# A decoder layer on one core: the norm of the retention outputs and the softmax each issued in two steps, and the key transposes in a step of their own

## The chip, the cores and the metric

The kernel runs on one core of one Trainium2 chip. A core has a matrix engine (TensorE, here PE, with its weight loads shown as PEld), a vector engine (DVE), an activation engine (ACT), a general engine (POOL), and SyncE (SP), which only issues transfers; they run side by side and meet through semaphores. The metric is the device time of one execution, in microseconds (us).

## The reference, cut to what matters

One decoder layer is computed for a prompt of 512 tokens and 8 samples of 8 tokens: 576 columns in all, D_MODEL 1024, fp32 throughout. After an RMS norm one combined projection gives the inputs of three branches, each with a norm, a scan or a softmax of its own; their projections are gated and merged, and an MLP and a small gated term follow. The two parts that the change touches are these:

```python
def step(s, inp):                      # retention, one chunk of 128 tokens
    qi, ki, vi = inp
    inner = einsum('bhid,bhjd->bhij', qi, ki) * dmask
    o = einsum('bhij,bhje->bhie', inner, vi) + einsum('bhid,bhde->bhie', qi * q_dec, s)
    s = s * c_dec + einsum('bhjd,bhje->bhde', ki * k_dec, vi)
    return s, o
...
o = o * lax.rsqrt(mean(o * o, axis=-1) + EPS)      # per head
return silu(rg) * o, s
...
m = maximum(max(s, axis=-1), sink)                 # window attention
pr = exp(s - m)
pr = pr / (sum(pr, axis=-1) + exp(sink - m))
```

## The kernel before, in words

Every large product is done in fp32 by splitting both operands into a high and a low part and adding three matmuls. Most of them go through `pair` or `pairs`: a recursive scheme with fewer multiplications whose `product` (L329) is 12 matmuls of 128x128 by 288 columns, accumulated in PSUM banks that the trace names pa, pbb and pe; the rest go through `unit` (`mm`, L501, bank pm). PE is fed with weights that SP loads (`wst`), ACT rounds (`whi`, L256 or L163), and DVE completes (`wlo`, L257 or L164; L227 first forms sums of weight blocks). Results leave PSUM through DVE (L424, L426) and ACT.

The branches' own small work runs in between. It is written as generators in a list `bg`; each `pump()` in `pair` and `unit` advances the first of them by one `yield`, so that a step's instructions are written between two big products. A framework then settles the order on each engine and the semaphores; within an engine that order is fixed. The banks for small work (tile pb) come from the same pool of six as pa and pe, so asking for a bank can wait for whoever reads the one that comes round next.

Retention (`ret_gen`) takes four prompt chunks of 128 tokens. For a chunk: scores (L713) with their decay mask (L717, DVE), transposed keys (L721, PE) with their decay (L723, DVE), decayed queries (L730, DVE, behind a POOL memset L728), outputs po (L737 from the scores and L739 from decayed queries and the state), state update pu (L744, L751). `ret_out` then normalises: squares on ACT, a mean over rows by a matmul (pn, L685), the inverse root (`rsqrt`: transpose L548, add L554, the power on POOL L555, refinement L556, L557, L560, transpose back L562), the gate t1 = po * rg (L690), and the product with the inverse root (L691). Convolution work (L838 to L845) and weight preparation share DVE with it. `stats` uses the same `rsqrt` at the start of the layer, once for each half of the columns; x is then normalised (L587, L653, L642) and made into operands for the pairs (L366, L583).

```python
yield
pk = bank("pb")                  # transposed keys: the bank that it gets is the last chunk's po
...
yield
yield
po = bank("pb")
...
yield
yield
pu = bank("pb")
```

Attention (`att_gen`) computes scores (L947, L952), `softmax` (maximum L892, exponentials L896 on ACT, denominator L899, L900, and eight scalings L902 on DVE), and the values (L972, L974, L964), block by block.

Of the kernel before, what the change touches and what calls it, by code (L numbers as in the profile page):

```python
# [10 lines left out]
ALU = mybir.AluOpType  # L11
AX = mybir.AxisListType

P = 128
# [70 lines left out]
def decoder_step(ctx: ExitStack, tc: tile.TileContext, xT, pT, W, consts, smalls, s0q, s0t, ckT, cv,  # L85
# [38 lines left out]
    def bank(s="ps"):  # L124
        return psum.tile([P, 512], F32, tag="ps", name=nm(s))
# [415 lines left out]
    def gain(i, k):  # L541
        return sm[:, S_G + 8 * i + k:S_G + 8 * i + k + 1]

    def rsqrt(v, w, out, c=1.0):

        nb = w // 32
        t1 = tmpt()
        V.transpose(t1[:, :w], v)  # L548
        tv = t1[:, :w].rearrange("p (b q) -> p b q", q=32)
        a = sml.tile([P, 18], F32, tag="rs_a", name=nm("rs_a"))  # L550
        b = sml.tile([P, 18], F32, tag="rs_b", name=nm("rs_b"))
        d = sml.tile([P, 18], F32, tag="rs_d", name=nm("rs_d"))
        a, b, d = a[:, :nb], b[:, :nb], d[:, :nb]
        V.tensor_scalar(a, tv[:, :, 0], EPS, None, op0=ALU.add)  # L554
        G.tensor_tensor(out=b, in0=a, in1=mhalf[:, :nb], op=ALU.pow)  # L555
        V.scalar_tensor_tensor(d, b, -0.5 * c, b, op0=ALU.mult, op1=ALU.mult)  # L556
        V.tensor_tensor(out=d, in0=d, in1=a, op=ALU.mult)  # L557
        t2 = t1
        t2v = t2[:, :w].rearrange("p (b q) -> p b q", q=32)
        V.scalar_tensor_tensor(t2v, d.unsqueeze(2).to_broadcast([P, nb, 32]), 1.5 * c,  # L560
                               b.unsqueeze(2).to_broadcast([P, nb, 32]), op0=ALU.add, op1=ALU.mult)
        V.transpose(out, t2[:, :w])  # L562

    def stats(sq_sum, rb, i):
        p = bank("pb")
# [111 lines left out]
    def ret_out(po, w, c0):  # L677

        ov = po[:, :4 * w]
        sq = bgtile()  # L680
        A.activation(sq[:, :4 * w], ov, AF.Square)
        yield
        yield
        pn = bank("pb")
        PE.matmul(pn[:, :4 * w], lhsT=ones_h, rhs=sq[:, :4 * w], start=True, stop=True)  # L685
        rs = bgtile()
        rsqrt(pn[:, :4 * w], 4 * w, rs[:, :4 * w], 0.5)
        t1 = bgtile()
        t1v = t1[:, :4 * w].rearrange("p (h i) -> p h i", h=4)
        V.tensor_tensor(out=t1v, in0=ov.rearrange("p (h i) -> p h i", h=4), in1=rg[:, :, c0:c0 + w], op=ALU.mult)  # L690
        V.tensor_tensor(out=ro[:, :, c0:c0 + w], in0=t1v,  # L691
                        in1=rs[:, :4 * w].rearrange("p (h i) -> p h i", h=4), op=ALU.mult)

# [3 lines left out]
    def odd(a, q):  # L697

        return a.rearrange("p (t q i) -> p t q i", t=2, q=2)[:, :, q, :]

    def ret_gen():
        vt = big.tile([P, 4, T], F32, tag="big", name="vt")
        state = None
        for c in range(4):
# [11 lines left out]
            for q in range(2):  # L716
                V.tensor_tensor(out=odd(st, q), in0=pst[q][:, :256].rearrange("p (t i) -> p t i", t=2),  # L717
                                in1=odd(cst[:, C_DMASK:C_DMASK + 512], q), op=ALU.mult)
            pk = bank("pb")
            for hp in range(2):  # L720
                PE.transpose(pk[:, 128 * hp:128 * hp + 128], rk[:, hp, cs], ident)  # L721
# [8 lines left out]
                    V.tensor_tensor(out=odd(qd, h)[hrow(h)], in0=rq[hrow(h), :, cs],  # L730
                                    in1=cst[hrow(h), C_QDEC:C_QDEC + 256].rearrange("p (t i) -> p t i", t=2), op=ALU.mult)
            yield
            yield
            po = bank("pb")
            for h in range(4):
                o = po[:, 128 * h:128 * h + 128]
                PE.matmul(o, lhsT=vc[:, 128 * h:128 * h + 128], rhs=st[:, 128 * h:128 * h + 128], start=True, stop=c == 0)  # L737
                if c:
                    PE.matmul(o, lhsT=state[:, h // 2, :], rhs=qd[:, 128 * h:128 * h + 128], start=False, stop=True)  # L739
            yield  # L740
            yield
            pu = bank("pb")
            for h in range(4):
# [142 lines left out]
    def softmax(sv, nh, sink):  # L886

        mx = mpool.tile([P, 8], F32, tag="mx", name=nm("mx"), bufs=2)[:, :nh]
        nmx = mpool.tile([P, 8], F32, tag="nmx", name=nm("nmx"), bufs=3)[:, :nh]
        den = mpool.tile([P, 8], F32, tag="den", name=nm("den"), bufs=3)[:, :nh]  # L890
        es = mpool.tile([P, 8], F32, tag="es", name=nm("es"), bufs=2)[:, :nh]
        V.tensor_reduce(out=mx, in_=sv, axis=AX.X, op=ALU.max)  # L892
        V.tensor_tensor(out=mx, in0=mx, in1=sink, op=ALU.max)
        V.tensor_scalar(nmx, mx, -1.0, None, op0=ALU.mult)
        for h in range(nh):
            A.activation(sv[:, h, :], sv[:, h, :], AF.Exp, bias=nmx[:, h:h + 1], accum_out=den[:, h:h + 1])  # L896
        V.tensor_tensor(out=es, in0=sink, in1=nmx, op=ALU.add)
        A.activation(es, es, AF.Exp)
        V.tensor_tensor(out=den, in0=den, in1=es, op=ALU.add)  # L899
        V.reciprocal(den, den)  # L900
        for h in range(nh):
            V.tensor_scalar(sv[:, h, :], sv[:, h, :], den[:, h:h + 1], None, op0=ALU.mult)  # L902

    def att_inputs():
        akv = bigt(F32, "akv")
# [18 lines left out]
    def att_gen(ak, av, avt, aq):  # L924
# [13 lines left out]
        def scores(n):  # L938
# [4 lines left out]
            for t in range(0, 4, 2):  # L943
# [8 lines left out]
                        V.scalar_tensor_tensor(s[:, h, :], dist, -SLOPES[h], p[g][:, i * w:i * w + w],  # L952
                                               op0=ALU.mult, op1=ALU.add)
                yield
            softmax(s, 8, sink)
            return s

        def values(n, s):
            nk = 1 if n == 0 else 2
# [29 lines left out]
                      in_=aq[:, :, NP:].rearrange("p t (b i) -> p t b i", b=8))  # L989
        yield  # L990
        sq = [bgtile()[:, :384].rearrange("p (n k) -> p n k", n=2) for _ in range(2)]
        for q in range(2):
            p = bank("pb")
            for n in (2 * q, 2 * q + 1):
# [6 lines left out]
                for j in range(4):  # L1001
# [7 lines left out]
            V.tensor_tensor(out=sq[q][:, :, 128:], in0=pq[:, :, 128:],  # L1009
                            in1=cst[:, C_ATTS + 128 + 128 * q:C_ATTS + 256 + 128 * q].rearrange("p (n k) -> p n k", n=2),  # L1010
                            op=ALU.add)
            softmax(sq[q], 2, sm[:, S_SINKS:S_SINKS + 1].to_broadcast([P, 2]))
            yield
        yield
        pt = bank("pb")
        for n in range(4):
# [24 lines left out]

        prev = None
        for n in range(4):
            s = yield from scores(n)
            if prev is not None:
                yield from values(n - 1, prev)
            prev = s
        yield from values(3, prev)

# [440 lines left out]
```

## Time and profile before

| what | value |
|---|---|
| time, median of 3 runs | 986.15 us (986.05 to 987.69) |
| the profiled execution: its time, its span | 987.22 us, 985.4 us |
| mean granted TensorE clock | 0.994 of full |
| busy in the span: PE, DVE, ACT, POOL | 957.6, 712.6, 531.5, 187.1 us |
| busy share: PE, DVE, ACT, POOL | 97%, 72%, 54%, 19% |
| chain of work that ended last, by engine | PE 77%, DVE 13%, DMA 4%, ACT 2% |

Busy is the time in which an engine had an instruction in work. The chain is followed back from the last instruction, at each step to what released it, so its shares say what set the end. A granted clock of 1 is 2.4 GHz and 0.5 is 1.2 GHz.

### The profile page before, as it was taken

The page shows a single profiled execution, that of the slowest core. Times are in us where ns is not written, and L with a number is a line of the kernel's source. Part 1 is how long each engine was busy: PE and PEld are TensorE (multiplying, and loading weights), DVE is VectorE, ACT ScalarE, POOL GpSimd, SP SyncE. Part 2 cuts the span into 40 slices and gives each one's busy share as a digit, 9 for nine tenths or more (in the row PEclk, how much of TensorE's full clock was granted, in tenths as well). Part 3 has the DMA queues.
Part 4 walks back from the last instruction along what each step waited for, and adds up shares of the span by engine and source line. Part 5 has one row for each costly group of instructions (what it writes and reads, how often), then busy time and mean ns, then how long its engine had stood idle before and what let it go on. Part 6 is the DMA issues. An engine that isn't in the chain of part 4 may idle for free.

```text
span 985.4 us, 18290 instructions
## 1 busy us (share of the span) xinstructions
PE 957.6 (97%) x7081; PEld 925.0 (94%) x7081; DVE 712.6 (72%) x1308; ACT 531.5 (54%) x1051; POOL 187.1 (19%) x257
## 2 busy tenths in 40 slices
PE   9999999989989999999999999999999999999998
PEld 9999898989979888799999999999999999999897
DVE  7898789765576776577427878558847965785986
ACT  7345444433345564545436455468558845885642
POOL 0414443433324222332001100000010011000010
PEclk9999999999999999999999999999999999999999
DMA  8637565658779665688522532444486368593112
GB/s 301 168 86 199 165 138 146 163 164 220 194 218 248 143 153 153 143 226 252 187 66 71 223 108 100 155 148 145 120 199 192 110 153 222 164 356 109 65 62 79
DMA packets 65576, 160.45 MB, mean 163 GB/s; under 512 B 8089, under 2 KB 11193, under 8 KB 64241
## 3 DMA queue, kind: packets, MB, share of 16 engines
q1 hardware_dynamic: 48672, 114.75, 34.9%
q0 software_dynamic: 16672, 44.48, 21.8%
q8 instruction: 55, 0.90, 0.4%
q14 instruction: 33, 0.26, 0.1%
q10 hardware_dynamic: 144, 0.06, 0.0%
HBM read 139.17 MB, written 51.55 MB: 194 GB/s over the span
## 4 chain that ended last, share of the span: by engine, by line
PE 77%; DVE 13%; DMA 4%; ACT 2%; issue 2%; POOL 1%; SPq 0%; ACTq 0%; DVEq 0%; POOLq 0%
PE pm L501 31%; PE pbb L329 18%; PE pa L329 12%; PE pe L329 12%; DMA wst<-in_W 3%; DVE wlo L257 3%; POOL rs_b L555 1%; DVE hlf L1149 1%; DVE xl L579 1%; DVE x L1150 1%; DVE wst L227 1%; DVE s L952 1%; PE pb L964 1%; ACT whi L256 1%; DVE wlo L164 1%
## 5 line engine op out<-in xcount | busy, mean ns | idle before, releaser
L257 DVE TENSOR_TENSOR wlo<-wst,whi 128x1024 fp32r<-128x1024 f32 (+1 forms) x180 | 195.4, 1087 | 95.9 <-ACT whi L256 95.1
L256 ACT CAST whi<-wst 128x1024 fp32r<-128x1024 f32 (+1 forms) x180 | 168.3, 940 | 129.9 <-PE pe L329 29.9
L329 PE MATMUL pbb<-xs,whi 128*128 128x288 f32 x1080 | 227.1, 302 | 10.0 <-DVE akv L426 4.1
L329 PEld LDWEIGHTS pbb<-xs,whi 128*128 128x128 f32 x1080 | 174.9, 190 | 19.0 <-DVE akv L426 4.9
L329 PE MATMUL pbb<-xs,wlo 128*128 128x288 f32 x540 | 160.6, 297 | 0.0
L329 PE MATMUL pa<-fq,whi 128*128 128x288 f32 x720 | 147.7, 297 | 0.6 <-DVE fq L583 0.5
L329 PEld LDWEIGHTS pa<-fq,whi 128*128 128x128 f32 x720 | 116.0, 189 | 2.3 <-DVE fq L583 0.7
L329 PE MATMUL pa<-fq,wlo 128*128 128x288 f32 x360 | 106.8, 297 | 0.4 <-DVE wlo L257 0.4
L329 PEld LDWEIGHTS pbb<-xs,wlo 128*128 128x128 f32 x540 | 102.7, 190 | 0.0
L163 ACT CAST whi<-wst 128x1024 fp32r<-128x1024 f32 (+1 forms) x64 | 61.5, 965 | 70.9 <-PE pm L501 48.8
L501 PE MATMUL pm<-xl,whi 128*128 128x288 f32 x384 | 95.0, 299 | 1.5 <-DVE xl L579 1.4
L501 PE MATMUL pm<-xh,whi 128*128 128x288 f32 x384 | 94.9, 300 | 1.5 <-ACT xh L578 1.4
L501 PE MATMUL pm<-xh,wlo 128*128 128x288 f32 x384 | 93.5, 296 | 0.3 <-DVE wlo L164 0.3
L164 DVE TENSOR_TENSOR wlo<-wst,whi 128x1024 fp32r<-128x1024 f32 (+1 forms) x64 | 71.2, 1118 | 23.7 <-ACT whi L163 21.3
L268 POOL COPY pace<-whi 128x1 f32<-128x1 f32 x61 | 36.6, 600 | 240.8 <-ACT whi L256 190.3
L227 DVE TENSOR_TENSOR wst<-wst 128x512 f32<-128x512 f32 x90 | 61.1, 686 | 28.7 <-DMA wst<-in_W 28.0
L555 POOL TENSOR_TENSOR rs_b<-rs_a,mhalf 128x9 f32<-128x9 f32 (+2 forms) x15 | 34.8, 2322 | 222.7 <-DVE rs_a L554 222.7
L329 PE MATMUL pe<-xs,whi 128*128 128x288 f32 x360 | 73.5, 294 | 0.1
L329 PE MATMUL pe<-fq,whi 128*128 128x288 f32 x360 | 73.3, 296 | 0.0
L501 PE MATMUL pm<-fq,whi 128*128 128x288 f32 x384 | 70.4, 296 | 0.0
L329 PEld LDWEIGHTS pa<-fq,wlo 128*128 128x128 f32 x360 | 67.9, 189 | 1.9 <-DVE wlo L257 1.1
L501 PEld LDWEIGHTS pm<-xh,whi 128*128 128x128 f32 x384 | 65.7, 188 | 3.9 <-ACT xh L578 2.4
(280 smaller groups left out, 2025.6 us busy)
## 6 DMA issues: line engine op xcount, KB each, us to landing
wst<-in_W SPq DMA_DIRECT2D x86, 512.0 KB, 4.5
wst<-in_W SPq DMA_DIRECT2D x105, 256.0 KB, 3.3
ts<-in_W POOLq DMA_DIRECT2D x90, 256.0 KB, 5.7
wst<-ts SPq DMA_DIRECT2D x60, 256.0 KB, 3.3
ts<-ts POOLq DMA_DIRECT2D x30, 256.0 KB, 3.5
df<-tmp POOLq DMA_DIRECT2D x16, 288.0 KB, 5.1
x<-in_xT SPq DMA_DIRECT2D x10, 288.0 KB, 4.2
dacc<-tmp SPq DMA_DIRECT2D x8, 288.0 KB, 4.3
```

What stands on the lines that cost most here:

```text
L163: A.copy(out=hi[:, c, :], in_=st[:, c, :])
L164: V.tensor_tensor(out=lo[:, c, :], in0=st[:, c, :], in1=hi[:, c, :].bitcast(F32), op=ALU.subtract)
L227: V.tensor_tensor(out=out, in0=a, in1=b, op=ALU.add)
L256: A.copy(out=hi, in_=r[:, :n, :])
L257: V.tensor_tensor(out=lo, in0=r[:, :n, :], in1=hi.bitcast(F32), op=ALU.subtract)
L268: t = G.tensor_copy(out=pace, in_=hi[:, 0, :1].bitcast(F32))
L329: PE.matmul(bank[:, :H], lhsT=lhs[:, s + j, :], rhs=rhs, start=start and j == 0 and i == 0, stop=j == 3 and i == 2, skip_group_check=True)
L501: PE.matmul(p[:, :H], lhsT=lhs[:, kw, :], rhs=r, start=s, stop=e)
L555: G.tensor_tensor(out=b, in0=a, in1=mhalf[:, :nb], op=ALU.pow)
L579: V.scalar_tensor_tensor(lo, src, gain(gi, k), hi.bitcast(F32), op0=ALU.mult, op1=ALU.subtract)
L952: V.scalar_tensor_tensor(s[:, h, :], dist, -SLOPES[h], p[g][:, i * w:i * w + w], op0=ALU.mult, op1=ALU.add)
L964: PE.matmul(po[grow(g), :], lhsT=avt[:, 128 * chunk + 64 * g:128 * chunk + 64 * g + 64], rhs=sb[g], start=kh == 0, stop=kh == nk - 1)
```

## The change: what it does

`rsqrt` becomes a generator, `rsqrt_steps`, that stops after the power on POOL; a wrapper `rsqrt` runs it through for `stats`. Its second half writes a tile of its own where it reused the first. `ret_out` runs the first half, then the gate t1, then yields, and does the second half in the next step. In `ret_gen` a `yield` stands ahead of the key transposes, and one is taken away ahead of po and one ahead of pu. `softmax` returns the denominator, the reciprocal and the scalings as a function, `probs()`, that the caller runs later.

```diff
-    def rsqrt(v, w, out, c=1.0):
+    def rsqrt_steps(v, w, out, c=1.0):
...
         G.tensor_tensor(out=b, in0=a, in1=mhalf[:, :nb], op=ALU.pow)
+        yield
         V.scalar_tensor_tensor(d, b, -0.5 * c, b, op0=ALU.mult, op1=ALU.mult)
         V.tensor_tensor(out=d, in0=d, in1=a, op=ALU.mult)
-        t2 = t1
+        t2 = tmpt()
...
+    def rsqrt(v, w, out, c=1.0):
+        for _ in rsqrt_steps(v, w, out, c):
+            pass
...
         rs = bgtile()
-        rsqrt(pn[:, :4 * w], 4 * w, rs[:, :4 * w], 0.5)
+        steps = rsqrt_steps(pn[:, :4 * w], 4 * w, rs[:, :4 * w], 0.5)
+        next(steps)
         t1 = bgtile()
         t1v = t1[:, :4 * w].rearrange("p (h i) -> p h i", h=4)
         V.tensor_tensor(out=t1v, in0=ov.rearrange("p (h i) -> p h i", h=4), in1=rg[:, :, c0:c0 + w], op=ALU.mult)
+        yield
+        for _ in steps:
+            pass
...
+            yield
             pk = bank("pb")
...
             yield
-            yield
             po = bank("pb")
...
-            yield
             yield
             pu = bank("pb")
...
-        V.tensor_tensor(out=den, in0=den, in1=es, op=ALU.add)
-        V.reciprocal(den, den)
-        for h in range(nh):
-            V.tensor_scalar(sv[:, h, :], sv[:, h, :], den[:, h:h + 1], None, op0=ALU.mult)
+
+        def probs():
+            V.tensor_tensor(out=den, in0=den, in1=es, op=ALU.add)
+            V.reciprocal(den, den)
+            for h in range(nh):
+                V.tensor_scalar(sv[:, h, :], sv[:, h, :], den[:, h:h + 1], None, op0=ALU.mult)
+        return probs
...
-            softmax(s, 8, sink)
-            return s
+            return s, softmax(s, 8, sink)
...
-            s = yield from scores(n)
+            s, probs = yield from scores(n)
             if prev is not None:
+                if n == 1:
+                    first_probs()
                 yield from values(n - 1, prev)
+                probs()
+            else:
+                first_probs = probs
```

The sample's softmax is split likewise: the scalings of its first half come after the scores of its second.

The new lines move the numbers: the power stays L555, L556 to L562 become L557 to L563, L587 L592, L690 (the gate) L696, L691 L700, L717 L726, L721 L731, L723 L733, L730 L740, L737 L746, L739 L748, L744 L752, L838 L846, L844 L852.

Order on DVE where the first chunk's norm stands (rs_a, rs_b, rs_d are the small tiles of the inverse root, L690 or L696 the gate). Before:

```order
L548 STREAM_TRANSPOSE tmp_1420<-pb_1417 128x512
L838 TENSOR_TENSOR ubuf_1455<-tmp_1146,tmp_1144 128x512
L554 TENSOR_SCALAR rs_a_1422<-tmp_1420 128x16
L839 TENSOR_TENSOR ubuf_1455<-tmp_1146,tmp_1144 128x8x8
L556 SCALAR_TENSOR_TENSOR rs_d_1424<-rs_b_1423 128x16
L557 TENSOR_TENSOR rs_d_1424<-rs_d_1424,rs_a_1422 128x16
L560 SCALAR_TENSOR_TENSOR tmp_1420<-rs_d_1424,rs_b_1423 128x512
L257 TENSOR_TENSOR wlo_1617<-wst_1611,whi_1616 128x1024
L562 STREAM_TRANSPOSE bgt_1419<-tmp_1420 128x512
L690 TENSOR_TENSOR bgt_1431<-pb_1276,rg_865 128x512
```

After, where the gate has already been done 8 rows above:

```order
L548 STREAM_TRANSPOSE tmp_1384<-pb_1381 128x512
L257 TENSOR_TENSOR wlo_1517<-wst_1420,whi_1516 128x1024
L554 TENSOR_SCALAR rs_a_1386<-tmp_1384 128x16
L426 TENSOR_TENSOR tmp_1149<-hlf_1340,pbb_1313 128x288
L557 SCALAR_TENSOR_TENSOR rs_d_1388<-rs_b_1387 128x16
L227 TENSOR_TENSOR wst_1650<-wst_1614 128x512
L558 TENSOR_TENSOR rs_d_1388<-rs_d_1388,rs_a_1386 128x16
L561 SCALAR_TENSOR_TENSOR tmp_1433<-rs_d_1388,rs_b_1387 128x512
L424 TENSOR_TENSOR tmp_1148<-pe_1314,hlf_1340 128x288
L563 STREAM_TRANSPOSE bgt_1383<-tmp_1433 128x512
L846 TENSOR_TENSOR ubuf_1458<-tmp_1148,tmp_1146 128x512
L700 TENSOR_TENSOR ro_1142<-bgt_1391,bgt_1383 128x4x128
```

The gate has gone from behind the refinement to ahead of the transpose; a large weight remainder (L257) now stands ahead of the add that starts the power, and one L227, one L424 and a convolution row have come in between the wait for the power and what follows it.

Order on DVE a little later in the same chunk, up to the decayed queries (bgt from rqk and cst, 64x2x128). Before:

```order
L838 TENSOR_TENSOR ubuf_1469<-tmp_1147,tmp_1145 128x512
L839 TENSOR_TENSOR ubuf_1469<-tmp_1147,tmp_1145 128x8x8
L723 TENSOR_TENSOR bgt_1538<-pb_1535,cst 128x256
L257 TENSOR_TENSOR wlo_1651<-wst_1647,whi_1650 128x1024
L844 SCALAR_TENSOR_TENSOR tmp_1468<-ubuf_1469,sm,tmp_1468 128x512
L844 SCALAR_TENSOR_TENSOR tmp_1468<-ubuf_1469,sm,tmp_1468 128x64
L845 SCALAR_TENSOR_TENSOR tmp_1468<-ubuf_1469,sm,tmp_1468 128x512
L845 SCALAR_TENSOR_TENSOR tmp_1468<-ubuf_1469,sm,tmp_1468 128x64
L730 TENSOR_TENSOR bgt_1540<-rqk_466,cst 64x2x128 x2
```

After:

```order
L726 TENSOR_TENSOR bgt_1535<-pb_1529,cst 128x2x128
L726 TENSOR_TENSOR bgt_1535<-pb_1530,cst 128x2x128
L852 SCALAR_TENSOR_TENSOR tmp_1471<-ubuf_1472,sm,tmp_1471 128x512
L852 SCALAR_TENSOR_TENSOR tmp_1471<-ubuf_1472,sm,tmp_1471 128x64
L853 SCALAR_TENSOR_TENSOR tmp_1471<-ubuf_1472,sm,tmp_1471 128x512
L853 SCALAR_TENSOR_TENSOR tmp_1471<-ubuf_1472,sm,tmp_1471 128x64
L880 TENSOR_TENSOR tmp_1457<-tmp_1457,pa_1485 128x288
L733 TENSOR_TENSOR bgt_1574<-pb_1571,cst 128x256
L257 TENSOR_TENSOR wlo_1654<-wst_1650,whi_1653 128x1024
L588 TENSOR_TENSOR cl_1144<-tmp_1457,ch_1143 128x288
L740 TENSOR_TENSOR bgt_1576<-rqk_468,cst 64x2x128 x2
```

A merge row (L880) stands ahead of the key decay, another row (L588) ahead of the decayed queries, and the decayed keys come just ahead of the last weight remainder where they stood ahead of the convolution rows.

Order on DVE at the start of the layer, where `stats` takes the inverse root of the two halves. Before:

```order
L556 SCALAR_TENSOR_TENSOR rs_d_421<-rs_b_420 128x9
L556 SCALAR_TENSOR_TENSOR rs_d_458<-rs_b_457 128x9
L227 TENSOR_TENSOR wst_699<-wst_699,wst_698 128x512
L557 TENSOR_TENSOR rs_d_421<-rs_d_421,rs_a_419 128x9
L557 TENSOR_TENSOR rs_d_458<-rs_d_458,rs_a_456 128x9
L560 SCALAR_TENSOR_TENSOR tmp_417<-rs_d_421,rs_b_420 128x288
L560 SCALAR_TENSOR_TENSOR tmp_454<-rs_d_458,rs_b_457 128x288
L562 STREAM_TRANSPOSE rb_128<-tmp_417 128x288
L562 STREAM_TRANSPOSE rb_128<-tmp_454 128x288
L587 TENSOR_TENSOR rqk_466<-pm_389,rb_128 128x288
L653 TENSOR_TENSOR rqk_466<-tmp_308,rb_128 128x576
```

After:

```order
L558 TENSOR_TENSOR rs_d_421<-rs_d_421,rs_a_419 128x9
L561 SCALAR_TENSOR_TENSOR tmp_426<-rs_d_421,rs_b_420 128x288
L548 STREAM_TRANSPOSE tmp_455<-pb_453 128x288
L563 STREAM_TRANSPOSE rb_128<-tmp_426 128x288
L554 TENSOR_SCALAR rs_a_457<-tmp_455 128x9
L592 TENSOR_TENSOR rqk_468<-pm_389,rb_128 128x288
L592 TENSOR_TENSOR rqk_468<-pm_483,rb_128 128x288
L557 SCALAR_TENSOR_TENSOR rs_d_459<-rs_b_458 128x9
L164 TENSOR_TENSOR wlo_621<-wst_619,whi_620 128x1024
L558 TENSOR_TENSOR rs_d_459<-rs_d_459,rs_a_457 128x9
L561 SCALAR_TENSOR_TENSOR tmp_464<-rs_d_459,rs_b_458 128x288
L563 STREAM_TRANSPOSE rb_128<-tmp_464 128x288
```

Before, the two halves went through the refinement side by side. Now the second half's transpose and power are started only behind the first half's refinement, and two rows of normalisation (L592) and the wait for the second power stand between.

## Rows read from the trace of the kernel before

**Rows 1.** The waits of PE: us in total, times, longest us.

```profile
PE pb L721 <- DVE bgt L690: 5.3, 2, 2.9
PE pbb L329 <- DVE akv L426: 4.1, 1, 4.1
PE pbb L329 <- DVE tmp L426: 3.5, 2, 2.9
```

**Rows 2.** Timeline of PE: start, us, line, tile, [idle before <- releaser].

```profile
62.25 0.40 PE L329 MATMUL pa<-fq,whi 128*128 128x288 f32 x1 [0.52 <-DVE fq L583]
...
118.39 0.69 PE L721 MATMUL pb<-cst,rqk 128*128 128x128 f32 x2 [2.42 <-DVE bgt L690]
...
150.16 0.44 PE L721 MATMUL pb<-cst,rqk 128*128 128x128 f32 x2 [2.92 <-DVE bgt L690]
...
209.44 0.54 PE L329 MATMUL pbb<-xs,whi 128*128 128x288 f32 x2 [2.90 <-DVE tmp L426]
```

**Rows 3.** Windows: us, PE, PEld, DVE, ACT, POOL busy, granted clock, DMA share, GB/s.

```profile
30.00:62.00 32.00, 31.74 (x237) 31.37 (x236) 31.55 (x66) 12.38 (x23) 9.85 (x16) 1.00 0.52 114
120.00:121.00 1.00, 1.00 (x6) 1.00 (x5) 1.00 (x5) 0.00 (x0) 0.00 (x0) 0.50 0.54 217
150.00:151.00 1.00, 0.84 (x7) 0.84 (x8) 1.00 (x4) 0.00 (x0) 0.00 (x0) 1.00 0.86 270
210.00:211.00 1.00, 1.00 (x6) 1.00 (x6) 0.99 (x5) 1.00 (x3) 0.00 (x0) 0.50 0.00 0
```

**Rows 4.** Timeline of DVE, around the norm of the first retention chunk.

```profile
114.89 0.17 DVE L556 SCALAR_TENSOR_TENSOR rs_d<-rs_b 128x16 f32<-128x16 f32 x1 [2.97 <-POOL rs_b L555]
...
117.68 0.65 DVE L690 TENSOR_TENSOR bgt<-pb,rg 128x512 f32<-128x512 f32 x1
...
121.23 0.69 DVE L838 TENSOR_TENSOR ubuf<-tmp,tmp 128x512 f32<-128x512 f32 x1
...
125.15 0.90 DVE L730 TENSOR_TENSOR bgt<-rqk,cst 64x256 f32<-64x256 f32 x2
```

**Rows 5.** Timeline of PE at the query-decay products of two chunks.

```profile
126.52 0.39 PE L739 MATMUL pb<-bgt,rstate 128*128 128x128 f32 x2
...
156.90 0.39 PE L739 MATMUL pb<-bgt,rstate 128*128 128x128 f32 x2
```

**Rows 6.** Timeline of POOL: powers, and the DMA issues ahead of one.

```profile
24.23 2.74 POOL L555 TENSOR_TENSOR rs_b<-rs_a,mhalf 128x9 f32<-128x9 f32 x1 [0.68 <-DVE rs_a L554]
...
28.87 1.80 POOL L555 TENSOR_TENSOR rs_b<-rs_a,mhalf 128x9 f32<-128x9 f32 x1 [1.90 <-DVE rs_a L554]
...
108.25 1.04 POOL L206 DMA_DIRECT2D ts<-in_W  x2
...
111.93 2.93 POOL L555 TENSOR_TENSOR rs_b<-rs_a,mhalf 128x16 f32<-128x16 f32 x1
...
142.80 3.34 POOL L555 TENSOR_TENSOR rs_b<-rs_a,mhalf 128x16 f32<-128x16 f32 x1 [2.09 <-DVE rs_a L554]
```

**Rows 7.** Timeline of DVE at the start of the layer.

```profile
24.05 1.22 DVE L164 TENSOR_TENSOR wlo<-wst,whi 128x1024 fp32r<-128x1024 f32 x1
...
31.20 0.24 DVE L556 SCALAR_TENSOR_TENSOR rs_d<-rs_b 128x9 f32<-128x9 f32 x2
...
32.90 0.83 DVE L562 STREAM_TRANSPOSE rb<-tmp 128x288 f32<-128x288 f32 x2
33.66 0.42 DVE L587 TENSOR_TENSOR rqk<-pm,rb 128x288 f32<-128x288 f32 x1
...
38.61 1.22 DVE L164 TENSOR_TENSOR wlo<-wst,whi 128x1024 fp32r<-128x1024 f32 x1
```

**Rows 8.** Timeline of DVE around the norm of the last prompt chunk.

```profile
190.76 1.23 DVE L257 TENSOR_TENSOR wlo<-wst,whi 128x1024 fp32r<-128x1024 f32 x1 [0.74 <-ACT whi L256]
...
196.10 1.42 DVE L227 TENSOR_TENSOR wst<-wst 128x512 f32<-128x512 f32 x2 [2.87 <-DMA wst<-in_W]
...
208.94 0.45 DVE L426 TENSOR_TENSOR tmp<-hlf,pbb 128x288 f32<-128x288 f32 x1
```

More of the change, by code (lines that the diff above doesn't have):

```diff
@@ L991, in att_gen @@
         sq = [bgtile()[:, :384].rearrange("p (n k) -> p n k", n=2) for _ in range(2)]
+        probs = []
         for q in range(2):
@@ L1011, in att_gen @@
                             op=ALU.add)
-            softmax(sq[q], 2, sm[:, S_SINKS:S_SINKS + 1].to_broadcast([P, 2]))
+            if probs:
+                probs.pop()()
+            probs.append(softmax(sq[q], 2, sm[:, S_SINKS:S_SINKS + 1].to_broadcast([P, 2])))
             yield
+        probs.pop()()
         yield
```

## Prediction

> **What bounds the kernel now.** The table of busy times comes first: PE works 957.6 of 985.4 us, so the change can win only what PE idles, some 28 us, and the time in which its clock is low. The list of PE's waits [rows 1] says for whom: twice for the gate L690 ahead of the key transposes, 5.3 us together, once for a DVE result of the projection behind it (akv, 4.1), and twice for another such result (tmp, 3.5, of which one is 2.9). PE's timeline puts three of these where the retention norms stand [rows 2]: 2.42 us before 118.39, 2.92 before 150.16, 2.90 before 209.44. In each the reader should see DVE as releaser, not a bank held by chance: the key transposes want po's bank, po is read last by the gate, and the gate stood behind the wait of DVE for the power on POOL, 2.97 us in the first chunk [rows 4]. The windows add a second price [rows 3]: after the waits of 2.42 and 2.90 PE ran at a granted clock of 0.50, 1.2 GHz, for about three windows of 1 us (the rows show one of each), so about 1.6 us were lost each time; after the wait of 2.92 it stayed at 1.00. An idle PE of this length can cost half as much again, but need not.
>
> **The change, chunk by chunk.** The gate now stands ahead of the transpose that begins the norm, and the transposed keys come two products later, so the waits of 2.42 and 2.92 us at the key transposes go: this is the sure part. What is late next is the decayed queries L740, which are on the same DVE behind the same power, and which PE needs at its products L748.
>
> *First chunk.* The power can't start before POOL has issued the two transfers ahead of it, at 108.25 + 1.04 = 109.3 [rows 6]; with 2.93 us [rows 6] and 0.1 on either side DVE goes on at 112.4, where it went on at 114.89 [rows 4]. From there to the end of the decayed queries DVE needed 125.15 + 0.90 - 114.89 = 11.2 us without a pause [rows 4]. In the new order that stretch loses the gate (0.6) and gains seven pieces: a block sum L227, a small weight remainder and the first convolution product (three of 128x512, each 0.6 by the start of L838 [rows 4] and its like), that product's short row (0.1), L424, L880 and L588 (0.4 each by the normalisation of the same size [rows 7]): 3.1 in all. The last L740 ends at 112.4 + 11.2 + 2.5 = 126.1. PE, without its wait and its slow stretch, would be at the first L748 at 126.52 - 2.42 - 1.6 = 122.5 [rows 2, 5]; it waits 3.6 us there, and goes on 0.4 us earlier than before. So the first wait is not removed but moved. If the clock falls behind it, up to 1.6 us more are lost, but DVE then gets as much ahead, and the next chunk gives it back.
>
> *Second chunk.* POOL is free from 142.80 - 2.09 = 140.7 [rows 6]; the power starts then, and at 2.93 ends at 143.7. Behind it I count, up to the end of L740: three large weight remainders of 1.1 (the start of L257 in [rows 8] to its end, less the overlap), ten rows of 128x512 of 0.6, four of 0.35, the L740 pair 0.9 and small ones 0.2: 11.8, so 155.6. PE's first L739 was at 156.90 [rows 5]; the gain so far is about 1.3.
>
> *Third chunk.* The same count gives L740 about 1.5 us earlier than PE needed it before. But here a large weight remainder is issued beside the power. The rows show what that does: with L164, the same form, beside it [rows 7], the power of 128x9 took 2.74, without it 1.80 [rows 6]; the power of 128x16 took 3.34 beside an L227 and 2.93 otherwise [rows 6]. I take 0.9 off: 0.6 us of gain stand after three chunks. The two ends are 1.5 (no lengthening) and 0 (it stretches the fourth chunk's too).
>
> The GPSIMD Engine Reference of the Trainium skill (section 1, Specifications) says that POOL shares its SBUF interfaces with the vector engine and that they contend when a vector instruction has two SBUF inputs; that speaks against putting vector work beside the power. The trace agrees: L164 and L227 have two SBUF inputs, and 2.74 stands against 1.80. Were it not so, the sum below would be 0.9 us better.
>
> *The wait before 209.44.* Here PE waited for L426, which began at 208.94 behind the norm of the fourth chunk [rows 8]; it would have had to end by 209.44 - 2.90 = 206.5. DVE came late to that norm because it waited 2.87 us for a weight transfer, to 196.10 [rows 8]. That transfer reuses the tile that the remainder at 190.76 reads, and is issued when it ends, at 191.9 [rows 8]. In the new order this remainder stands ahead of the merge rows and behind the state update, whose product comes two products earlier; I put its end at 189 to 190. So the transfer lands 2 to 3 us earlier, the gate (0.65, [rows 4]) is out of the way as well, and L426 ends at 205 to 206: PE doesn't wait, and saves 2.90 + 1.6 for the slow stretch behind it [rows 2, 3] = 4.5. If the transfer does not come earlier, L426 ends near 208.0, and hardly anything is won. I take the 4.5, since what the transfer waits for is moved.
>
> *The start.* `stats` runs the inverse root without a break for each half, but its second half now writes a tile of its own, and the order has changed: the second half's transpose and power are started behind the first half's refinement. Before, both were refined together from 31.20, and the last transpose ended near 33.7 [rows 7]. Now the first half's rows are through near 32.5 (32.90 less one of its rows, [rows 7]); two transposes and the add (0.4 + 0.4 + 0.1) bring the second power to start at 33.5, and at 1.80 [rows 6] it ends near 35.3. Two normalisations (0.8, [rows 7]) are all that covers it. Then the refinement, with the L164 that stood at 38.61 pulled in between, ends near 37.7; the old order would have had the same work done at 33.7 + 0.8 + 1.15 = 35.6. DVE is 2.1 us late. From 30 to 62 it is busy 31.55 of 32.00 us [rows 3], so 0.4 us are absorbed, and PE already waited 0.52 us for it at 62.25 [rows 2]: the cost is 1.7. The ends: 0.5, if only the late transposes count, and 2.1 + 1.6 = 3.7, if the clock falls behind a wait that is now over 2 us.
>
> *The rest.* The softmax split moves eight scalings per block (DVE) past scores of the next block; PE's list shows no wait of a microsecond there, and no term of the sum stands on it: 0, with 0.5 either way. The wait of 4.1 for akv [rows 1] belongs to a weight transfer ahead of which DVE's order hardly changes: 0.
>
> **The sum.** Chunks 0.6, the wait at 209 4.5, the start -1.7: 3.4 us faster than the profiled execution's 987.2, so 983.8. That execution was 1.1 us above the median of 986.15; on the median's scale I predict 982.8.
>
> **Rivals.** (1) *All that waited is gone*: the three waits and two slow stretches, 2.42 + 2.92 + 2.90 + 3.2 = 11.4, less the start: about 976. It needs DVE to be quicker than its own rows from 112.4 on, and it ran without a pause there [rows 4]. (2) *The gain is moved, not made*: L748 takes the place of L721 and the transfer of 196.10 comes when it came. Then 0.6 - 1.7 gives 987.2, and with a mild start 986: no change, which is what a difference under 0.2%, 2.0 us, has to be called here. For it speaks that the remainder at 190.76 itself waited for ACT [rows 8]; against it, that DVE's own rows stood ahead of both. (3) *The start costs more than the chunks win*: DVE is the bound from 30 to 62, the wait at 62.25 grows from 0.52 to 2.2, the clock falls behind it, and the start alone costs 3.3; with the 209 wait left as it was, 0.6 - 3.3 gives 988.9. It decides from the point at which the second power ends more than 2 us after the second L592, with no saving at 209.
>
> **Chances.** Forecast 0.47, rival 1 0.08, rival 2 0.29, rival 3 0.16. The range from 978.8 to 988.3 leaves out rival 1 and the far part of rival 3; the forecast's own goes from 980.7 to 984.8 (the ends of the start, and the better one of the third chunk). Faster by over 0.2% are the forecast, all but its last part, and rival 1: 0.53; within it rival 2 and that part: 0.30; slower 0.17.
>
> **What would show it.** Right: no wait for the gate at L731; a new wait of PE at L748 for L740 of 2 to 4 us in the first chunk, shorter ones in the second and third; no wait of PE for L426 near 205 and one slow stretch less; the wait near 62 grown to about 2.2; the DVE wait at the second L557 of the start about 1 us. Wrong: L740 in time in the first chunk (then rival 1), or the L227 near 193 still waiting for its transfer until 196 (then rival 2). The prediction fails if the order in which engines meet is disturbed by transfers that now start earlier and collide, of which no row here speaks.

## The result, and the profile after

The change makes the kernel slower: 991.79 us median of 20 runs (988.34 to 998.37) against 986.22 before (983.29 to 988.58), a ratio of 1.0056 with an interval of 1.0043 to 1.0068, where 982.8 was predicted. The profiled execution took 989.42 us, with a span of 987.7 and a mean clock of 0.995. The runs of the change spread more than those of before, and with the clock: those at 0.995 took 988.3 to 989.4 us, those at 0.987 995.5 and 998.4.

PE's list of waits after, as in [rows 1] (us in total, times, longest):

```profile
PE pbb L329 <- DVE tmp L426: 5.2, 2, 2.7
PE pb L748 <- DVE bgt L740: 4.8, 3, 2.9
PE pbb L329 <- DVE akv L426: 2.7, 1, 2.7
...
PE pbb L329 <- DVE aq L426: 1.9, 1, 1.9
```

The waits for the gate at the key transposes (5.3 us) are gone. L748 now waits for the decayed queries (4.8), L426 has two waits of over 2 us for tmp where it had one, and one for aq is new. PE's timeline shows where, as in [rows 2]:

```profile
62.87 0.40 PE L329 MATMUL pa<-fq,whi 128*128 128x288 f32 x1 [1.57 <-ACT fq L587]
64.24 0.40 PE L329 MATMUL pa<-fq,whi 128*128 128x288 f32 x1 [0.97 <-DVE fq L588]
...
114.03 0.54 PE L329 MATMUL pbb<-xs,whi 128*128 128x288 f32 x2 [2.47 <-DVE tmp L426]
...
160.21 0.49 PE L748 MATMUL pb<-bgt,rstate 128*128 128x128 f32 x2 [2.86 <-DVE bgt L740]
...
189.58 0.49 PE L748 MATMUL pb<-bgt,rstate 128*128 128x128 f32 x2 [1.76 <-DVE bgt L740]
...
214.06 0.85 PE L329 MATMUL pbb<-xs,whi 128*128 128x288 f32 x2 [2.68 <-DVE tmp L426]
```

At 62 to 64 PE now waits 1.57 + 0.97 where it waited 0.52 [rows 2]: it is 2.0 us behind from there on. At 114 and at 214 it waits for L426, at 160 and 189 for L740. The windows say what the clock did around three of these, as in [rows 3]:

```profile
115.00:116.00 1.00, 1.00 (x6) 1.00 (x6) 0.00 (x0) 0.00 (x0) 1.00 (x1) 0.50 0.53 193
161.00:162.00 1.00, 1.00 (x11) 1.00 (x10) 1.00 (x4) 0.00 (x0) 0.00 (x0) 1.00 0.70 231
214.00:215.00 1.00, 0.94 (x4) 0.94 (x5) 0.97 (x3) 0.75 (x2) 0.00 (x0) 0.50 0.05 16
```

It fell at the waits of 2.47 and 2.68, and not at that of 2.86. The same kernel, profiled again (the run e4_change_again below), had it the other way at this wait, in its timeline of PE:

```profile
162.38 0.49 PE L748 MATMUL pb<-bgt,rstate 128*128 128x128 f32 x2 [2.89 <-DVE bgt L740]
```

The window behind it, in the same profile:

```profile
164.00:165.00 1.00, 1.00 (x7) 1.00 (x6) 1.00 (x3) 0.00 (x0) 0.00 (x0) 0.50 0.06 20
```

So which wait is followed by low clock changes from run to run. What held L426 up in the first chunk is on DVE's timeline after (as in [rows 4]):

```profile
109.90 1.29 DVE L227 TENSOR_TENSOR wst<-wst 128x512 f32<-128x512 f32 x2 [3.31 <-DMA wst<-in_W]
...
111.71 0.71 DVE L548 STREAM_TRANSPOSE tmp<-pb 128x512 f32<-128x512 f32 x1
...
113.53 0.45 DVE L426 TENSOR_TENSOR tmp<-hlf,pbb 128x288 f32<-128x288 f32 x1
116.66 0.18 DVE L557 SCALAR_TENSOR_TENSOR rs_d<-rs_b 128x16 f32<-128x16 f32 x1 [2.69 <-POOL rs_b L555]
```

DVE stood 3.31 us at a block sum L227 for a weight transfer. Behind that row, in order, came the norm's transpose, a remainder, the add, and only then L426, at 113.53, for which PE had been waiting since 111.6. The power came last: PE's wait here is not the power's, since the wait of DVE of 2.69 for POOL follows it. It has two parts, the late transfer and the norm's rows that now stand ahead of L426; the experiments with the gate alone and with everything but the tile tell them apart below. The fourth chunk, in the same view, has both (as in [rows 8]):

```profile
194.16 1.23 DVE L257 TENSOR_TENSOR wlo<-wst,whi 128x1024 fp32r<-128x1024 f32 x1
...
201.54 1.42 DVE L227 TENSOR_TENSOR wst<-wst 128x512 f32<-128x512 f32 x2 [3.85 <-DMA wst<-in_W]
...
208.94 0.18 DVE L557 SCALAR_TENSOR_TENSOR rs_d<-rs_b 128x16 f32<-128x16 f32 x1 [2.84 <-POOL rs_b L555]
...
213.56 0.45 DVE L426 TENSOR_TENSOR tmp<-hlf,pbb 128x288 f32<-128x288 f32 x1
```

The remainder at 194.16 lets the transfer be issued, DVE waits for it to 201.54, then for the power to 208.94, and L426 starts at 213.56.

### The profile page after: what moved, and what is told of

Its sections match the earlier page's. It is cut to its first block, busy times and chain, and to the rows that moved or that the text cites. A ratio compares the mean times of both kernels' runs of the same rounds, so it can differ in the third digit from the quotient of the medians.

```text
span 987.7 us, 18282 instructions
## 1 busy us (share of the span) xinstructions
PE 957.7 (97%) x7081; PEld 924.2 (94%) x7081; DVE 713.2 (72%) x1308; ACT 531.8 (54%) x1051; POOL 189.2 (19%) x257
## 4 chain that ended last, share of the span: by engine, by line
PE 71%; DVE 17%; DMA 5%; issue 3%; ACT 3%; POOL 2%; ACTq 0%; POOLq 0%; DVEq 0%; SPq 0%
PE pm L501 29%; PE pbb L329 16%; PE pa L329 11%; PE pe L329 10%; DMA wst<-in_W 5%; DVE wlo L257 3%; POOL rs_b L555 2%; DVE wst L227 2%; DVE hlf L1168 1%; DVE xl L584 1%; DVE wlo L164 1%; DVE x L1169 1%; DVE stmp L366 1%; ACT s L904 1%; PE pb L974 1%
## 5 line engine op out<-in xcount | busy, mean ns | idle before, releaser
L257 DVE TENSOR_TENSOR wlo<-wst,whi 128x1024 fp32r<-128x1024 f32 (+1 forms) x180 | 195.7, 1088 | 94.0 <-ACT whi L256 92.7
L227 DVE TENSOR_TENSOR wst<-wst 128x512 f32<-128x512 f32 x90 | 61.2, 687 | 26.2 <-DMA wst<-in_W 25.4
L555 POOL TENSOR_TENSOR rs_b<-rs_a,mhalf 128x9 f32<-128x9 f32 (+2 forms) x15 | 35.6, 2370 | 225.2 <-DVE rs_a L554 225.1
L501 PEld LDWEIGHTS pm<-xl,whi 128*128 128x128 f32 x384 | 65.5, 188 | 3.7 <-DVE xl L584 3.3
```

The source lines that it names most:

```text
L227: V.tensor_tensor(out=out, in0=a, in1=b, op=ALU.add)
L257: V.tensor_tensor(out=lo, in0=r[:, :n, :], in1=hi.bitcast(F32), op=ALU.subtract)
L501: PE.matmul(p[:, :H], lhsT=lhs[:, kw, :], rhs=r, start=s, stop=e)
```

## The experiments

Twelve runs were made, three of them of a kernel that had been run already (the change, the kernel before, the gate alone), each timed beside the kernel before on the same chip; ratios are to that. A ratio here is not the quotient of the two medians beside it; in each run that quotient lies inside the interval given. Two theories stood against each other: A, that the start pays (the two halves of the first norm one after the other), and B, that the retention steps pay, since what is moved comes back as another wait.

**A tile of its own, nothing else.**

```diff
-        t2 = t1
+        t2 = tmpt()
```

> The kernel before with one edit: the second half of the inverse root writes a tile of its own. Theory A (the start pays: with the second tile the two halves of the first norm are refined one after the other, which put PE 1.98 us behind at 63 us in the profile after): 2 to 4 us slower than before, 988.2 to 990.2, PE late by about 2.0 us at its first product of the pairs, and more runs with extra stretches of low clock. Theory B (the retention steps pay: waits of PE behind weight transfers that land late): within 1 us of before, 985.2 to 987.2.

Measured: 988.86 against 986.37 us, ratio 1.0020 (1.0001 to 1.0038). DVE at the start stood as in the change (its timeline):

```profile
33.42 0.13 DVE L554 TENSOR_SCALAR rs_a<-tmp 128x9 f32<-128x9 f32 x1
33.53 0.82 DVE L587 TENSOR_TENSOR rqk<-pm,rb 128x288 f32<-128x288 f32 x2
35.50 0.17 DVE L556 SCALAR_TENSOR_TENSOR rs_d<-rs_b 128x9 f32<-128x9 f32 x1 [1.15 <-POOL rs_b L555]
35.61 1.23 DVE L164 TENSOR_TENSOR wlo<-wst,whi 128x1024 fp32r<-128x1024 f32 x1
...
37.44 0.48 DVE L562 STREAM_TRANSPOSE rb<-tmp 128x288 f32<-128x288 f32 x1
```

The second power is started after 33.42, two normalisations cover part of it, DVE waits 1.15 us, and the second half's transpose ends near 37.9. So one line that looks like bookkeeping costs about 2 us (0.1 to 3.7 by the interval) by the order that it brings about. Theory A holds for this part. What PE loses there has two parts. In this profile it waits 0.83 + 0.98 us at its first products of the pairs, 1.3 more than before, and a stretch of half the clock follows, from 65.9 to 69.3. Of the four profiles with the new tile (this one, the change twice, the change without the power) three have low clock there; of the ten without it none has.

**Everything but the tile.**

```diff
-        t2 = tmpt()
+        t2 = t1
```

(against the change)

> The whole change, but the second half of the inverse root reuses the first tile as before. Theory A: the start is as before, so 1 us faster to 1 us slower than before, 985 to 987. Theory B: the retention steps alone make it about as slow as the change, 990 to 992, with PE waits for L426 and L740 of over 2 us in the chunks and a mean clock of 0.989 to 0.993 in most runs.

Measured: 989.25 against 986.37, ratio 1.0036 (1.0023 to 1.0050). Theory A alone fails, and B's 990 to 992 is missed by 0.8 us on the faster side. 0.20% and 0.36% add up to the change's 0.56%; with intervals of 0.19 and 0.14 on either side the exact agreement is chance, but the start and the chunks both cost time. PE waits 2.53 us for L426 at 111.85 and 2.85 and 1.77 for L740, all as in the change, with the start undisturbed. The clocks of the runs didn't give what B had expected: their mean is 0.9930, that of before 0.9931.

**The softmax alone.** The diff is the softmax part of the change.

> The kernel before with the softmax split alone. Both theories: 0 to 1 us faster than before, 985.2 to 986.2, since PE made good 0.8 us between 322 and 397 us in the profile after. If it is more than 1 us slower, the softmax is a third cause.

Measured: 986.87 against 986.37, ratio 1.0001 (0.9987 to 1.0015): nothing that can be told, where 0 to 1 us of gain was expected.

**The change once more.**

> The changed kernel once more, for its spread: median 990.8 to 992.8. If stretches of low clock make the spread, a run's time rises by about 1 us for each 0.001 that its mean clock falls (3.4 us at half the clock, seen in both profiles, lose 1.7 us and 0.0017 of the mean); if transfers make it, time spreads at equal clock. Profile: the same waits, but other ones of them followed by low clock.

Measured: 993.68 (990.58 to 996.47, 6 runs), ratio 1.0068 (1.0043 to 1.0092); the median is above the 990.8 to 992.8 that were expected. The profiled run, with a span of 994.1 us and a clock of 0.987, had the same waits (23.6 us of PE's idle time in all, against 24.3) and more low clock.

**The gate alone.**

```diff
-        rs = bgtile()
-        rsqrt(pn[:, :4 * w], 4 * w, rs[:, :4 * w], 0.5)
         t1 = bgtile()
...
         V.tensor_tensor(out=t1v, ...)
+        rs = bgtile()
+        rsqrt(pn[:, :4 * w], 4 * w, rs[:, :4 * w], 0.5)
```

> The kernel before with the gate t1 = po * rg written ahead of the inverse root; root in one piece, no yield moved, softmax as before. Order on DVE is that of before but for the gate. Theory A (the gate is what the key transposes waited for, and the rest of the change cost the gain): the two waits of 2.4 and 2.9 us at the key transposes go; PE then waits up to 3.5 us for the decayed queries in the first chunk and not in the second; 2 to 4 us faster, 982.4 to 984.4. Theory B (whatever moves in the chunks comes back as another wait behind the power and the weight transfers): within 1 us of before.

> The gate alone once more, to narrow its interval: 0.1 to 0.25% faster than before, as in the first run of it (0.9984); if that was chance, within 0.1%.

Measured: 985.00 against 986.38, ratio 0.9984 (0.9965 to 1.0002), and again 986.92 against 986.48, 0.9997 (0.9981 to 1.0012): no difference that can be told, so the 0.16% of the first time was chance by the second expectation, and A's 2 to 4 us are missed. The waits for the gate went, as A said; PE then waited at the query products and for L426 (its list of waits):

```profile
PE pbb L329 <- DVE tmp L426: 6.4, 4, 2.5
PE pb L739 <- DVE bgt L730: 4.5, 2, 2.9
```

This run also prices the order ahead of L426 in the first chunk, where the gate alone leaves it as it was. The same weight transfer ends DVE's wait at 107.69 here (DVE's timeline, the gate alone):

```profile
107.69 0.69 DVE L227 TENSOR_TENSOR wst<-wst 128x512 f32<-128x512 f32 x1 [1.34 <-DMA wst<-in_W]
...
110.16 0.45 DVE L426 TENSOR_TENSOR tmp<-hlf,pbb 128x288 f32<-128x288 f32 x1
```

and at 107.72 in everything but the tile (its DVE timeline):

```profile
107.72 1.29 DVE L227 TENSOR_TENSOR wst<-wst 128x512 f32<-128x512 f32 x2 [3.37 <-DMA wst<-in_W]
...
111.35 0.45 DVE L426 TENSOR_TENSOR tmp<-hlf,pbb 128x288 f32<-128x288 f32 x1
```

With the transfer at the same time, L426 starts 1.2 us later in the new order, and PE waits 2.53 us for it where it waits 1.06 with the gate alone. The change itself has the same 3.63 us from that row to L426 (109.90 to 113.53). So of its wait of 2.47 about 1.2 is the order, and the rest the transfer.

**The yields alone**, and **the split alone.** The first moves the three yields of the chunk and leaves norm and gate; the second splits the root with the gate between the steps and leaves the yields.

```diff
+            yield
             pk = bank("pb")
...
-            yield
             po = bank("pb")
...
-            yield
             pu = bank("pb")
```

> The kernel before with the yields alone: one ahead of the key transposes, one less ahead of the outputs and ahead of the state update. Theory A: the key transposes come 3.2 us later on PE, so their waits for the gate shrink by about that, but the norm starts earlier and its power holds L426: 0 to 2 us faster, 984.4 to 986.4. Theory B: the waits come back at L426 and at the decayed queries, as in the change: 2 to 4 us slower, 988.4 to 990.4.

> The kernel before with the root in two steps and the gate between them (first tile reused, no yield moved in the chunk generator, softmax as before). Theory A: as with the gate alone, 2 to 4 us faster, 982.4 to 984.4. Theory B: 2 to 4 us slower as the second run of this study.

Measured: 996.84 against 986.38, ratio 1.0100 (1.0081 to 1.0119), and 991.76, 1.0041 (1.0023 to 1.0060). The yields alone are worse than both together with the softmax (1.0036 above), by far more than either theory had expected; the split alone isn't told apart from that. With the yields alone the waits are for L426 (7.9), for the gate (4.3) and for the scores (2.9), in PE's list:

```profile
PE pbb L329 <- DVE tmp L426: 7.9, 3, 2.9
PE pm L501 <- DVE bgt L690: 4.3, 1, 4.3
PE pb L737 <- DVE bgt L717: 2.9, 1, 2.9
```

With the split alone they are for L426 on three tiles, 14 us together, in PE's list:

```profile
PE pbb L329 <- DVE tmp L426: 8.1, 3, 4.1
PE pbb L329 <- DVE aq L426: 4.1, 2, 3.0
PE pbb L329 <- DVE hlf L426: 2.1, 1, 2.1
```

In each the reader sees another row of DVE that PE waits for, and never the power itself. B holds in kind: the waits move. Its size, 2 to 4 us, holds at best for the split (5.4 us between the medians, 4.0 by the ratio), and not for the yields (10.5).

**Without the power.** The retention norms take a reciprocal on DVE in place of the power on POOL, so their values are others; the norm of the start and the later ones keep the power. Once on the change, once on the kernel before:

```diff
-        G.tensor_tensor(out=b, in0=a, in1=mhalf[:, :nb], op=ALU.pow)
+        if w == H:
+            G.tensor_tensor(out=b, in0=a, in1=mhalf[:, :nb], op=ALU.pow)
+        else:
+            V.reciprocal(b, a)
```

> The whole change, with the power of the retention norms replaced by a reciprocal on DVE (so the norm's values are others; the norm of the start keeps the power). If the wait of DVE for POOL is what makes PE wait in the chunks, the waits for L740 (2.9 and 1.8) and for L426 at 214 (2.7) go: 4 to 7 us faster than the change, 985 to 988. If the weight transfers make them, DVE still waits 2 to 4 us at L227, the waits for L426 stay at 1.5 to 2.5, and it is within 2 us of the change, 990 to 993.

> The kernel before with the power of the retention norms replaced by a reciprocal on DVE (other norm values, as in the run before). If the power is what all its chunk waits hang on, the waits of 2.4, 2.9 and 2.9 us for the gate and for L426 go, with two stretches of low clock: 6 to 9 us faster than before, 977 to 980, and the change without the power (979.5) has nothing left to win against it. If moving the gate and the yields is worth something of its own, this one stays 3 us or more above 979.5.

Measured: 979.49 against 986.38, ratio 0.9919 (0.9897 to 0.9941), for the change without the power, faster than either range that was expected; 975.06 against 986.48, 0.9870 (0.9847 to 0.9893), for the kernel before without it, faster than the 977 to 980 expected. Two waits for DVE of over 0.5 us are left in the chunks on PE's timeline of the change without the power (L743 and L751 are L740 and L748 there):

```profile
114.61 0.69 PE L329 MATMUL pbb<-xs,whi 128*128 128x288 f32 x2 [2.42 <-DVE tmp L426]
...
129.97 0.38 PE L751 MATMUL pb<-bgt,rstate 128*128 128x128 f32 x1 [0.70 <-DVE bgt L743]
```

DVE's timeline ahead of the first of them:

```profile
110.47 1.29 DVE L227 TENSOR_TENSOR wst<-wst 128x512 f32<-128x512 f32 x2 [3.26 <-DMA wst<-in_W]
```

Of the waits for L740 0.9 us is left (4.8 with the power), 0.70 of it here, and PE waits no more for L426 where it did at 214. L426 in the first chunk still waits 2.42, and DVE ahead of it 3.26 for the transfer: that one isn't the power's. In the kernel before without the power no wait for the gate is left, and again one for L426 in the first chunk (the head of PE's list that bears on it):

```profile
PE pbb L329 <- DVE tmp L426: 2.2, 2, 2.0
PE pbb L329 <- ACT pe L400: 1.5, 2, 1.0
```

The kernel before gains 11.4 us by losing the power, the change 12.3; and with the power out of both, the change is still 4.4 us slower than before. The last two differences are between medians that were not measured side by side; the ratios, each beside before, give 13.5 and 4.8. So most of the chunk waits that it was to avoid hung on the power, and the change costs something beside them; about 2 us of that is the start, whose norm kept its power in both. Without the power POOL is also free for its transfers earlier; no run separates that from DVE's wait.

**The gate and the decayed queries ahead of the norm.** The gate as above, and the queries L730 of the next chunk made before the norm is issued:

```diff
-            if c:
-                qd = bgtile()
...
+            if c < 3:
+                qd = decayed(slice(128 * c + 128, 128 * c + 256))
             yield from ret_out(po, 128, 128 * c)
```

> The kernel before with the gate ahead of the root, and the decayed queries of the next chunk made ahead of the norm as well, so that nothing that PE needs at po stands behind the power. If the waits at the query products (2.9 and 1.6 us in the run with the gate alone) are what is left of the gain, they go: 3 to 6 us faster than before, 980.4 to 983.4. If they come back at L426 once more, within 1.5 us of the gate alone, 983.5 to 986.5.

Measured: 983.89 against 986.48, ratio 0.9966 (0.9950 to 0.9982): it beats both kernels, by 2.6 us against before between the medians, less than the 3 that were expected at least; 983.89 lies in the range set for waits that come back at L426. The waits at the query products are gone from PE's list:

```profile
PE pbb L329 <- DVE tmp L426: 5.4, 4, 2.0
PE pbb L329 <- DVE akv L426: 3.9, 1, 3.9
...
PE pbb L329 <- DVE hlf L426: 1.8, 1, 1.8
```

PE still waits 5.4 and 1.8 us for L426 on two tiles, three of the longer waits (1.78 at 127.46, 1.45 at 157.89, 1.96 at 208.71) behind a norm, and one (1.25 at 111.03) behind a weight transfer.

**The kernel before, as a kernel of its own.**

> The kernel before, run as a kernel of its own, for the clock of its runs: ratio 1.000 within 0.1%. If the change costs time by low clock, the mean clock here is 0.993 to 0.995 in most runs where the change had 0.989 to 0.993; if by its waits alone, both have the same clocks.

Measured: 986.76 against 986.48, ratio 0.9990 (0.9972 to 1.0008). Its mean clock was 0.9936 over 12 runs, that of the runs of before beside it 0.9931 over 26; the change had 0.9911 over 20, and 0.9907 over the 6 of its second time.

**What the profiles have in common.** For each, PE's idle time is summed over its waits of 0.2 us and more, and the time at half the clock (without the last microseconds, where PE is done) is counted half:

| kernel | span | PE waits | low clock | span - waits - low/2 |
|---|---|---|---|---|
| before, twice | 985.4, 985.2 | 22.4, 20.7 | 10.2, 13.7 | 957.9, 957.7 |
| the change, twice | 987.7, 994.1 | 24.3, 23.6 | 6.8, 23.9 | 959.9, 958.6 |
| tile alone; all but the tile | 987.4; 987.3 | 21.8; 21.1 | 13.7; 13.7 | 958.8; 959.4 |
| yields alone; split alone | 994.7; 988.3 | 25.5; 22.9 | 23.9; 13.7 | 957.2; 958.6 |
| softmax alone | 983.8 | 17.8 | 17.1 | 957.5 |
| gate alone, twice | 984.6, 985.6 | 22.0, 20.5 | 6.8, 13.7 | 959.2, 958.3 |
| gate and queries | 981.8 | 19.5 | 6.8 | 958.9 |
| no power: change; before | 978.0; 972.3 | 15.0; 11.3 | 6.8; 3.4 | 959.6; 959.3 |

What is left is 957 to 960 us in every kernel, nearly all of it PE's own work. Most of what differs is how long it waits and how much low clock there is, but not all: the two profiles of the change are 1.5 us above the two of before in the last column, and no run shows why. Where a stretch of low clock begins inside a wait, half of that part is counted twice, 1.3 us at most (the yields alone), and that doesn't account for it.

## Why the prediction was wrong, step by step

Three terms failed. The largest, 4.5 us for the wait before 209.44, was not gained; the powers of the first two chunks started 4.4 and 3.1 us later than the sum had them; and L426 behind the first norm's rows, priced at nothing, cost 1.2 us. The rows behind DVE's wait for the power took what had been counted for them in both chunks.

*That the waits for the gate go, and that L748 waits for L740 in their place*: right; 0 of 5.3 is left, and 4.8 are new. The sizes and the places were off: 3.6 us were put in the first chunk, where hardly any came, since PE had been held at 114.03 already; the second and third have 2.86 and 1.76.

*The first chunk*: here a step failed. "The power can't start before POOL has issued the two transfers ahead of it" gave 109.3; it began at 113.70, because DVE, not POOL, was late: the norm's transpose stands behind a block sum, and that waited 3.31 us for its weight transfer. POOL's own wait says so (its timeline after):

```profile
113.70 2.93 POOL L555 TENSOR_TENSOR rs_b<-rs_a,mhalf 128x16 f32<-128x16 f32 x1 [3.54 <-DVE rs_a L554]
```

From DVE's next row, at 116.66, to the end of L740, at 130.24, it is 13.6 us, where 11.2 + 2.5 were counted: the rows were right, the start was 4.3 late. The prediction named the wait of DVE for a weight transfer only in the fourth chunk. And it costed L426, which now stands behind the norm's first rows, at nothing; the two runs above put it at 1.2 us. This transfer had 512 KB; its median time from issue to landing stands last in the list of transfers, first of before (100 to 102 us):

```profile
wst<-in_W SPq DMA_DIRECT2D x1, 512.0 KB, 4.4
```

And of after (102 to 105 us):

```profile
wst<-in_W SPq DMA_DIRECT2D x1, 512.0 KB, 6.2
```

It took 4.4 and 6.2 us. Why, stays open: both lists have two of POOL's transfers of 256 KB beside it, and no run changed these alone. The 4.4 was the shortest of all fourteen profiles; before, profiled again, had 5.5, and the others 5.1 to 7.9. So a part of this lateness is the luck of the one profile that the prediction was read from. It was also issued later, at 103.64 in place of 101.21; with everything but the tile, where the start is undisturbed, it was issued at 101.26 and took 6.4.

*The second chunk*: that POOL is free from 140.7 and that "the power starts then" failed too. The power began at 143.83. POOL issued two transfers up to 143.72 (its timeline after), and the add that the power reads began on DVE at 143.58:

```profile
142.07 1.65 POOL L204 DMA_DIRECT2D ts<-in_W  x2
```

Behind it DVE waited once more for a weight transfer ahead of the decayed queries (DVE's timeline after):

```profile
156.94 0.69 DVE L227 TENSOR_TENSOR wst<-wst 128x512 f32<-128x512 f32 x1 [1.78 <-DMA wst<-in_W]
...
159.75 0.86 DVE L740 TENSOR_TENSOR bgt<-rqk,cst 64x256 f32<-64x256 f32 x2
```

L740 ended at 160.6 where 155.6 was predicted: 3.1 us from the late power, 1.8 from the transfer. The rows between, counted at 11.8, took 12.0. With everything but the tile, where the start is undisturbed, the wait of PE is the same (2.85), so the late start of the layer doesn't make it.

*The second and third chunk*: the power beside a large remainder was taken at 0.9 longer; it took 3.63 in the third chunk, against 2.93 without in the second (POOL's timeline after):

```profile
143.83 2.93 POOL L555 TENSOR_TENSOR rs_b<-rs_a,mhalf 128x16 f32<-128x16 f32 x1
...
173.30 3.63 POOL L555 TENSOR_TENSOR rs_b<-rs_a,mhalf 128x16 f32<-128x16 f32 x1
```

So 0.7 was the price. The GPSIMD Engine Reference of the Trainium skill (section 1, Specifications) names the cause, an SBUF interface shared with vector instructions that have two SBUF inputs; the trace agrees with its direction, and the number is this row's.

*The wait before 209.44*, the largest term (4.5): this failed. That "the transfer lands 2 to 3 us earlier" rested on the remainder ending at 189 to 190; it ended at 195.4, as all ahead of it was late (the start 2.0, the first chunk, and L740), and the transfer then took 6.1 us instead of 4.1 (from the lists of transfers, first of before, 191.9 to 192.6 us):

```profile
wst<-in_W SPq DMA_DIRECT2D x1, 512.0 KB, 4.1
```

And of after (194 to 196 us):

```profile
wst<-in_W SPq DMA_DIRECT2D x1, 512.0 KB, 6.1
```

Here the profiles agree on what goes with it. Before, this transfer is issued at 192.01, between two of POOL's at 191.97 and 192.51; after, at 195.42, behind both (194.59 and 195.14). In the eight profiles with the first order it took 3.5 to 4.1 us, in the six with the second, all of kernels with yields moved or the root split, 4.6 to 6.1. No run changed the order of issue alone. L426 started at 213.56, and 2.68 us of wait and the low clock behind it remained. That a wait goes because its release is moved ahead in the order holds only if nothing ahead of that is later.

*The start*: right in place, and near in price on the average. 1.7 us were predicted; PE is 2.0 us behind at 64 us in the first profile of the change, and the tile alone costs 0.20%. But the forecast had no low clock there and kept it for the end of its range at 3.7, and three of the four profiles with the new tile have it. The wait at the second L557 was to be about 1 us; it was 1.15.

*The softmax and akv*: the split is worth nothing, as said. For akv, PE waited 2.7 us where it had waited 4.1, but before, profiled again, also had 2.3: this wait varies with the run.

*The clock*: the sum counted one stretch of low clock less. The change has more: mean clock 0.991 against 0.993 (the runs of before beside the experiments), two thousandths of 987 us, or some 2 us; over the 20 runs of the change the time falls by about 0.8 us for each thousandth. Together with PE's waits, 2.4 us more on the average of two profiles each, this is some 4.4 of the measured 5.6; the rest is of the size of the 1.5 us by which the last column of the table differs, and stays open.

The rival on the slower side was priced at 988.9: 3.3 lost at the start, low clock included, less 0.6 gained in the chunks. The tile alone costs 2.0 (0.20%), and the chunks cost 3.6 (0.36%) where they were to gain. So no rival had the cost of the chunks.

## What to carry to other kernels

A short wait of an in-order engine for another engine (here some 3 us for a power) is a hole through which everything behind it falls: moving the row that is seen to wait only shows the next one, so list every row behind the hole that somebody waits for, and move all of them or fill the hole (here moving one gave nothing that can be told, moving two 0.34%). Before a moved row is priced at its new place, look at what that place itself waits for: here a weight transfer stood ahead of it. And an edit that seems to touch no order, a second buffer, can serialise two chains that ran side by side; read the order, and cost it.

## What the runs showed of the hardware that was not expected

Whether a PE wait of 2.5 to 3 us is followed by a stretch at half the clock differs from run to run of one kernel: 2.86 us at L748 was not followed by one, 2.89 at the same place in the next profile was. The length of the wait alone doesn't decide it: this one, in PE's timeline of the change's second profile, was followed by one (0.50 from 194 to 195):

```profile
193.32 0.49 PE L748 MATMUL pb<-bgt,rstate 128*128 128x128 f32 x2 [1.77 <-DVE bgt L740]
```

The wait of 3.0 for aq with the split alone was not (1.00 from 288 to 290). Each stretch of 3.4 us loses up to 1.7, and two profiles with nearly the same waits lie 6.4 us apart (24.3 us of waits in a span of 987.7, 23.6 in 994.1), so a single profile can't tell what a change does to this kernel by its span.
